# Fourteen seven-product pairs per group in a hybrid decoder layer, with attention work moved into the shared stretch

## The chip, the cores and the metric

The kernel runs on one core of one Trainium2 chip. The metric is the device time of one execution in microseconds (us): 1808.11 us is the median of three runs before (1805.93 to 1808.54). Engines are named as in the profile: PE is TensorE (PEld its weight loads), DVE VectorE, ACT ScalarE, POOL GpSimd, SP SyncE, whose queue issues nearly all transfers.

## The reference

One decoder layer on 256 tokens and 16 prepended meta tokens (272 rows), model width 4096, all in 32-bit floats:

```python
h = rmsnorm(x, norm_g)                        # (272, 4096)
q, k, v, g_attn, b, c, hc, z = split(h @ w_in)  # w_in (4096, 16384)
o = stick_breaking_attention(q, k, v)         # 16 heads of 128, strictly causal
o = group_rmsnorm(o * silu(g_attn), ...)      # per head
y = b * short_conv(c * hc, conv_w)            # width 3, causal
y = group_rmsnorm(y * silu(z), ...)           # per channel group
out = rmsnorm(x + concat(o, y) @ w_out, final_norm_g)   # w_out (4096, 4096)
```

In the attention a query t gives key s the weight sigmoid(z_ts) times the product over the keys between them of (1 - sigmoid), summed up in log space. Nearly all of the arithmetic is the two projections.

## The kernel before, in words

**Numbers.** Every 32-bit operand is split into a high part (a cast to the fast matmul format, on ScalarE) and a low part (operand minus high part, on VectorE), and a product is three matmuls: high by low, high by high, low by high. Weights arrive by DMA as pieces of 128 x 1024 (512 KB, tile `raw`, five buffers); `split` makes `wh` (L401) and `wl` (L397) of each, in rings of six buffers (`RING`), five pieces ahead of TensorE; `load` issues transfers eight pieces ahead. A cast into the ring therefore waits until TensorE has finished the piece six before it.

**Pieces and groups.** The list `pieces` is the order of the work, written out by `in_pieces` and the loop behind it. The input projection goes in eight groups, each of two heads and two channel groups. Of the eight kinds of columns four (k, v, c, hc) are made with the weights standing and the tokens moving: a block `("p", (unit, kind), kc)` of four pieces of 24 matmuls over 272 or 258 columns (L434 to L436), accumulated in one PSUM bank. The other four (q, g_attn, b, z) are made as a 2 x 2 block product: tokens split in two halves, columns in two halves of 512, and the 32 chunks of the width taken as 16 pairs j. A plain pair has two pieces A and B, eight products, 24 matmuls of 512 columns (L442 to L445), accumulated in four banks D11, D12, D21, D22. A shared pair (`seven`) uses a seven-product scheme of the Strassen kind: 21 matmuls, in four pieces A, B, T, U, where T and U are sums of weight halves that VectorE makes (L418, L421, L423) and that are split as well; it accumulates into D11, D12, D21 and four more banks P1, P5, P7, P6. It also needs split sums of the tokens: those of the pairs in `HELD` stay in SBUF, those of `LENT` are made once in group 0 (`late_sums`), stored to DRAM, and read back in every group into two buffers (`lent`).

**Stretches.** A group begins with a plain stretch (zone "R"): its plain pairs, with the last blocks of the group before in between. The four extra banks are then free for the attention of the group before (`spare`). Then D22 is complete and copied out (`open_rows`), and the shared stretch (zone "S") follows: shared pairs, each with half a block behind it, all eight banks in use but the one that D22 left, which holds the block in progress (`block_bank`) and, between two blocks, one other product. Group 0 has plain pairs only. At the end of a group `evict` combines the eight banks into four row tiles.

**Tasks.** Everything else is a task at a position in the list of pieces: `later(at, fn)` files it and `run_tasks(i)` emits it behind piece i, so each engine's queue order is written out by hand. A task that yields k continues k pieces later. `plan_group` places, for group g with f its last block piece in the shared stretch: the gates (`silu`), the transposes of q (`q_t`), `scores`, and for each of two heads `weights` (logarithms, scans, exponentials), `trans` (a transpose in 32 x 32 blocks on VectorE, then sixteen copies of 32-row blocks by `blocks`, alternately on ScalarE and VectorE, L575 and L573) and `po` (the product with v, then an eviction on VectorE); and in the shared stretch of the next group, at `slot`s (piece B of a shared pair), the convolution's transposes (`conv_t`, `conv_out`), `squares`, `norm` and `mix`, which scales, transposes and stores the mixed rows to DRAM.

**Output projection.** Four groups (8 to 11) of 1024 columns (the last 768) are made the same way from the mixed rows, which come back from DRAM as pieces `("m", group)`; `MIXED` and `OUT_FIRST` say where. Their shared pairs are 8 to 13 (the first group: 8 to 11), and the token sums for them are made by `kept_sums`, with the four sums on GpSimd (L308 to L311) in `raw_sums`. `out_sums` and `out_blocks` add the products to the residual rows and square them. The last 256 columns are pieces `("o", 8, kc)` (L933 to L935), then the final norm (`finish`).

Of the kernel before, what the change touches and what calls it, by code (L numbers as in the profile page):

```python
# [15 lines left out]
P = 128  # L16
# [34 lines left out]
MIXED = {(1, "A"): 2, (3, "A"): 3, (5, "A"): 4, (6, "B"): 5, (9, "A"): 6}  # L51
# [7 lines left out]
def sevens(g):  # L59

    return OUT_SJ[:4] if g == GROUPS else OUT_SJ if g > GROUPS else SJ if g else ()

# [5 lines left out]
def in_pieces():  # L68
# [14 lines left out]
    first = ((0, 0), (0, 1), (0, 2), (0, 3), (1, 0), (1, 1))  # L83
    last = ((1, 2), (1, 3))
# [17 lines left out]
    for i, t in enumerate(blocks_of(GROUPS - 1, last)):  # L102
        block(*t)
        if i in (1, 3):
            out.append(("m", i // 2))
# [9 lines left out]
def kernel(ctx, tc, xt, xin, xm, par, fg, w1, w2, out):  # L115
# [23 lines left out]
    ones = wk.tile([P, P], F32, tag="zl", name="ones")  # L139
# [23 lines left out]
    for g in range(GROUPS, GROUPS + 4):  # L163
        for at_, j in enumerate(OUT_ORDER if g > GROUPS else OUT_FIRST):
            for q in "ABTU" if seven(g, j) else "AB":
                pieces.append((q, g, j))
                if g == GROUPS and (at_, q) in MIXED:
                    pieces.append(("m", MIXED[at_, q]))
        fin[g] = len(pieces) - 1
# [111 lines left out]
    def late_sums(j):  # L281
# [6 lines left out]
        yield 2  # L288
# [6 lines left out]
    def kept_sums(d, t, j):  # L295

        f = raw_sums(t, f"o{j}")
        yield 2
# [4 lines left out]
    def raw_sums(t, j):  # L303
# [3 lines left out]
        v = nc.gpsimd  # L307
# [23 lines left out]
    def load(i):  # L331
# [16 lines left out]
        elif p[0] == "m":  # L348
# [12 lines left out]
    def split(i):  # L361
# [9 lines left out]
        if p[0] == "m":  # L371
            t = raws.pop(i).rearrange("p (a b) -> p a b", a=4)
            h, lo = mixh[p[1]], mixl[p[1]]
            nc.scalar.copy(out=h, in_=t)
            for q in range(2):
                j = 2 * p[1] + q
                if j in OUT_SJ:
                    if j < 12:
                        S2[j] = fgs["pool"].tile([P, 2, 4, P], F32R, tag=f"keep{j - 8}", name=f"osum{j}")
                    else:  # L380
                        S2[j] = wk.tile([P, 2, 4, P], F32R, tag="cq" if j == 12 else "cb0", name=f"osum{j}")
                    later(now[0], kept_sums, S2[j], t[:, 2 * q:2 * q + 2], j)
# [95 lines left out]
    def mm_in(i):  # L478
        p = pieces[i]
        if p[0] in "xm":  # L480
            return
# [16 lines left out]
    def block_bank(i):  # L498
# [5 lines left out]
        if kind == "Z":  # L504
            return d + 2 * ((2 * u + b) % 2)
        return d + D22 if g else (4, 5, 6, 0, 1, 2)[{(0, 0): 0, (0, 1): 1, (0, 2): 2, (0, 3): 3, (1, 0): 4, (1, 1): 5}[u, b]]

    def spare(i):
# [5 lines left out]
        if kind == "Z":  # L514
            return [d + 3, d + 1]
# [22 lines left out]
    def finish_stats():  # L538
# [13 lines left out]
        x, y, t = (wk.tile([P, L], F32, tag=q, name=f"st{q}", bufs=2 if q == "u2" else 1) for q in ("u2", "zl", "kT1"))  # L552
# [11 lines left out]
    def blocks(dst, src, n, half):  # L564
# [3 lines left out]
        for i in (0, 1) if half == 0 else (2, 3):  # L568
            for j in range(4):
                o = d[32 * j:32 * j + 32, :, 32 * i:32 * i + 32]  # L570
                x = s[32 * i:32 * i + 32, :, 32 * j:32 * j + 32]
                if (i + j) % 2:
                    V.tensor_copy(out=o, in_=x)  # L573
                else:
                    A.copy(out=o, in_=x)  # L575
# [9 lines left out]
    def v_block(u, src, at_):  # L585
# [4 lines left out]
        def vtrans():  # L590
# [4 lines left out]
            blocks(vv, y[:, :2 * P], 2, 0)  # L595
            yield 1
            blocks(vv, y[:, :2 * P], 2, 1)
# [12 lines left out]
    def h_block(u, src, at_):  # L610
# [3 lines left out]
        def conv():  # L614
            V.tensor_tensor(out=c, in0=c, in1=rstd[:, META - 2:], op=ALU.mult)
            y = wk.tile([P, SEQ], F32, tag=f"cy{u % 2}", name=f"cy{u}")
            w = [pt[:, CW0 + 3 * u + i:CW0 + 3 * u + i + 1] for i in range(3)]
            V.tensor_scalar(out=y, in0=c[:, 0:SEQ], scalar1=w[0], scalar2=None, op0=ALU.mult)
# [6 lines left out]
    def plain_block(u, b, e):  # L625
# [7 lines left out]
        else:  # L633
            h_block(u, ps[:, META - 2:L], after(e, 1))
# [110 lines left out]
    def scores(g):  # L745
# [8 lines left out]
        for u in range(2):  # L754
            zm[u] = (wk.tile([P, 512], F32, tag="u2", name=f"zm{g}_{u}", bufs=2) if u else
                     wk.tile([P, 448], F32, tag="zm", name=f"zm{g}_{u}"))[:, :ZW]
            l[u] = wk.tile([P, 448], F32, tag="kT0" if u else "zl", name=f"zl{g}_{u}")[:, :ZW]
# [86 lines left out]
    def plan_group(g):  # L844
# [4 lines left out]
        later(after(f, 1), q_t, g)  # L849
        later(after(f, 2), silu, g, "c")  # L850
        later(after(f, 3), scores, g)
        for u, at_ in enumerate(((6, 8, 11), (8, 10, 14))):
            for k, fn in zip(at_, (weights, trans, po)):
                later(after(f, k), fn, g, u)
        later(after(f, 16), squares, g, "h")
        if end:
            later(after(e, 4), conv_t, (2 * g, 2 * g + 1))
            later(after(e, 6), conv_out, g)
            later(after(f, 17), squares, g, "c")
            later(after(f, 18), norm, g)  # L860
            later(after(f, 20), mix, g, "h")
            later(after(f, 21), mix, g, "c")
# [133 lines left out]
    for q, j in enumerate(LENT):  # L996
        later(after(top[0], 3 * q + 1), late_sums, j)
# [148 lines left out]
```

## Time and profile before

| | |
|---|---|
| median of three runs | 1808.11 us |
| the profiled execution, its own time | 1808.45 us |
| its span, first to last instruction | 1806.7 us |
| granted TensorE clock, mean | 0.996 |
| PE, DVE, ACT, POOL busy | 99%, 86%, 62%, 8% |
| matmuls of the blocks (L434 to L436) | 6144 |
| moved by DMA | 393.64 MB |

A row of a group of instructions reads: line, engine, operation, tile written <- tiles read, shape, count | busy us, mean ns of one | idle time of the engine before them and what ended it. A row of a timeline reads: start, length, engine and line, with the idle time before it in brackets. A row of waits reads: total us, times, longest. A row of stretches gives the length, the busy time of each engine with its instructions in brackets, the granted clock as a share of full speed, and the DMA's share and rate. Matmuls are pipelined, so that the length of one is more than the step to the next.

### The profile page before, as it was taken

How to read it: one execution, taken by the hardware profiler on the slowest of the kernel's cores; microseconds unless marked ns; L12 is line 12 of the kernel's file. 1: busy time of each engine (PE TensorE's matmuls, PEld its weight loads, DVE VectorE, ACT ScalarE, POOL GpSimd, SP SyncE). 2: the span in 40 equal slices, each digit the busy share in tenths (PEclk: the TensorE clock that was granted, in tenths of full speed). 3: DMA queues.
4: the chain of work that ended last, by engine and by line, in shares of the span. 5: the costliest groups of instructions: out<-in, count | busy, mean ns of one | idle time of the engine just before them, and what ended most of it. 6: DMA issues, size and time to landing. Idle time of an engine off the chain costs nothing.

```text
span 1806.7 us, 29670 instructions
## 1 busy us (share of the span) xinstructions
PE 1784.4 (99%) x11004; PEld 1618.5 (90%) x11004; DVE 1555.5 (86%) x2104; ACT 1120.3 (62%) x1736; POOL 144.5 (8%) x192
## 2 busy tenths in 40 slices
PE   9999999999999999999999999999999999999996
PEld 7899999999998999899999999999999987888896
DVE  6776899889988998899889988998899889898985
ACT  6755666666676667566756575667566765555553
POOL 2132010001000101010101010101010142000000
PEclk9999999999999999999999999999999999999998
DMA  8876567756775676567656765676567666676664
GB/s 311 310 255 209 176 210 236 229 176 212 236 229 172 215 243 211 184 216 236 212 185 216 240 218 172 215 244 218 171 220 244 208 209 238 200 242 213 203 221 162
DMA packets 116065, 393.64 MB, mean 218 GB/s; under 512 B 13008, under 2 KB 18256, under 8 KB 115920
## 3 DMA queue, kind: packets, MB, share of 16 engines
q1 hardware_dynamic: 111888, 388.08, 65.0%
q10 hardware_dynamic: 4032, 3.67, 0.6%
q8 instruction: 86, 1.41, 0.3%
q14 instruction: 59, 0.48, 0.1%
HBM read 380.17 MB, written 11.53 MB: 217 GB/s over the span
## 4 chain that ended last, share of the span: by engine, by line
PE 93%; DVE 3%; ACT 1%; POOL 1%; DMA 1%; issue 1%; SPq 0%; DVEq 0%; POOLq 0%; ACTq 0%
PE P L442 16%; PE P L445 16%; PE P L444 16%; PE mm L436 13%; PE mm L435 13%; PE mm L434 13%; DVE wl L397 1%; DMA raw<-w 1%; ACT wh L401 1%; PE mo L933 0%; PE mo L935 0%; PE mo L934 0%; POOL sfo L308 0%; PE z L752 0%; PE po L808 0%
## 5 line engine op out<-in xcount | busy, mean ns | idle before, releaser
L397 DVE TENSOR_TENSOR wl<-raw,wh 128x1024 fp32r<-128x1024 f32 (+2 forms) x754 | 849.3, 1147 | 121.6 <-ACT wh L401 110.8
L401 ACT CAST wh<-raw 128x1024 fp32r<-128x1024 f32 (+2 forms) x754 | 714.1, 976 | 379.6 <-PE mm L435 109.4
L434 PE MATMUL mm<-xs,wh 128*128 128x258 f32 (+1 forms) x2048 | 582.7, 285 | 0.0
L435 PE MATMUL mm<-xs,wh 128*128 128x258 f32 (+1 forms) x2048 | 581.8, 284 | 0.0
L436 PE MATMUL mm<-xs,wl 128*128 128x258 f32 (+1 forms) x2048 | 581.6, 284 | 0.0
L435 PEld LDWEIGHTS mm<-xs,wh 128*128 128x128 f32 x2048 | 385.6, 188 | 4.1
L434 PEld LDWEIGHTS mm<-xs,wh 128*128 128x128 f32 x2048 | 385.5, 188 | 4.1
L436 PEld LDWEIGHTS mm<-xs,wl 128*128 128x128 f32 x2048 | 385.6, 188 | 0.0
L442 PE MATMUL P<-wh,xs 128*128 128x512 f32 x604 | 238.6, 395 | 1.5 <-ACT wh L401 1.5
L445 PE MATMUL P<-wl,xs 128*128 128x512 f32 x604 | 235.5, 390 | 0.2
L444 PE MATMUL P<-wh,xs 128*128 128x512 f32 x604 | 235.4, 390 | 0.0
L401 ACT CAST wh<-t 128x1024 fp32r<-128x1024 f32 (+1 forms) x106 | 110.4, 1042 | 171.7 <-DVE t L418 97.3
L442 PE MATMUL P<-wh,mixl 128*128 128x512 f32 (+1 forms) x402 | 152.2, 379 | 2.5 <-ACT wh L401 2.5
L445 PE MATMUL P<-wl,mixh 128*128 128x512 f32 (+1 forms) x402 | 151.8, 378 | 0.5 <-DVE wl L397 0.5
L444 PE MATMUL P<-wh,mixh 128*128 128x512 f32 (+1 forms) x402 | 151.5, 377 | 0.0
L445 PEld LDWEIGHTS P<-wl,xs 128*128 128x128 f32 x604 | 113.4, 188 | 25.2 <-DVE wl L397 1.1
L442 PEld LDWEIGHTS P<-wh,xs 128*128 128x128 f32 x604 | 113.5, 188 | 22.7 <-ACT wh L401 1.8
L444 PEld LDWEIGHTS P<-wh,xs 128*128 128x128 f32 x604 | 113.5, 188 | 19.5
L418 DVE TENSOR_TENSOR t<-raw,raw 128x1024 f32<-128x1024 f32 (+1 forms) x106 | 129.7, 1223 | 0.2
L397 DVE TENSOR_TENSOR wl<-t,wh 128x1024 fp32r<-128x1024 f32 (+1 forms) x106 | 129.6, 1222 | 0.0
L442 PEld LDWEIGHTS P<-wh,mixl 128*128 128x128 f32 x402 | 75.7, 188 | 15.1 <-ACT wh L401 3.0
L445 PEld LDWEIGHTS P<-wl,mixh 128*128 128x128 f32 x402 | 75.7, 188 | 13.2 <-DVE wl L397 1.3
(248 smaller groups left out, 2017.8 us busy)
## 6 DMA issues: line engine op xcount, KB each, us to landing
raw<-w SPq DMA_DIRECT2D x614, 512.0 KB, 4.3
lent<-sumd SPq DMA_DIRECT2D x49, 512.0 KB, 6.0
raw<-w SPq DMA_DIRECT2D x32, 384.0 KB, 3.9
raw<-xin SPq DMA_DIRECT2D x8, 512.0 KB, 5.7
xr<-xt SPq DMA_DIRECT2D x15, 272.0 KB, 5.5
sumd<-lent SPq DMA_DIRECT2D x7, 512.0 KB, 4.3
raw<-mixd SPq DMA_DIRECT2D x7, 512.0 KB, 4.1
res<-xin SPq DMA_DIRECT2D x12, 256.0 KB, 4.8
```

The costliest lines, as they stand in the source:

```text
L397: nc.vector.tensor_tensor(out=lo[:, c], in0=t[:, c], in1=h[:, c].bitcast(F32), op=ALU.subtract)
L401: nc.scalar.copy(out=h[:, c], in_=t[:, c])
L418: nc.vector.tensor_tensor(out=s[:, :2 * hw].rearrange("p (a b) -> p a b", a=2), in0=a[:, :2 * hw].rearrange("p (a b) -> p a b", a=2), in1= ...
L434: nc.tensor.matmul(out=o, lhsT=h, rhs=x[:, 0, s:], start=k == 0, stop=False)
L435: nc.tensor.matmul(out=o, lhsT=h, rhs=x[:, 1, s:], start=False, stop=False)
L436: nc.tensor.matmul(out=o, lhsT=lo, rhs=x[:, 0, s:], start=False, stop=k == KC - 1)
L442: nc.tensor.matmul(out=o, lhsT=a[1], rhs=h, start=key not in begun, stop=False)
L444: nc.tensor.matmul(out=o, lhsT=a[0], rhs=h, start=False, stop=False)
L445: nc.tensor.matmul(out=o, lhsT=a[0], rhs=lo, start=False, stop=last)
```

## The change

- Groups 1 to 7 make 14 of the 16 pairs shared instead of 12: pairs 3 and 9 join, in `LENT`, and the order `SJ` of the shared pairs changes. The plain stretch has two plain pairs (0 and 12) instead of four. In the first output group two pairs (9, 10) are shared instead of four.
- Seven of a group's eight blocks (instead of six) lie in its shared stretch, one in the next plain stretch. The scores' logarithm of the second head has a buffer of its own (`zl1` for `kT0`).
- `plan_group`: q's transposes and the scores come one piece later; the first head's weights and transpose stay near, the second head's weights come at f+9; both products `po`, the second head's `trans` and the squares of the attention's half go to slots of the next shared stretch, in the free bank; convolution, norm and mixing move to later slots. The last group has its own places.
- `blocks` copies one 32-column quarter per piece, on ScalarE alone, for v and for the weights (the last group's weights: both engines, two quarters at once). The convolution's first multiply goes from VectorE to ScalarE, and of even units the convolution starts eight pieces after its block.
- The sums of the mixed rows for the output's shared pairs are made on VectorE (`raw_sums(..., V)`). The sums of pairs 12 and 13 are made in the second output group from a second load of mixed rows 6 (piece "k").
- The output groups have an order each (`OUT_ORDERS`); the mixed rows and the residual are loaded at other places. The sums for lent pairs start 2.5 instead of 3 pieces apart, and their cast comes one piece later.

```diff
-LENT = (2, 5, 8, 11, 14, 15, 6)
-SJ = (2, 1, 5, 4, 8, 7, 11, 10, 14, 13, 15, 6)
-OUT_ORDER = (0, 1, 2, 3, 8, 4, 9, 5, 10, 6, 11, 7, 12, 13, 14, 15)
-OUT_FIRST = (0, 1, 2, 3, 4, 5, 6, 8, 7, 9, 14, 10, 15, 11, 12, 13)
+LENT = (2, 5, 8, 11, 14, 15, 6, 3, 9)
+SJ = (2, 1, 5, 4, 8, 11, 7, 14, 15, 10, 6, 13, 3, 9)
+OUT_ORDERS = (
+    (0, 1, 2, 3, 4, 5, 6, 7, 8, 9, 12, 14, 10, 15, 11, 13),
+    (0, 1, 2, 3, 8, 4, 9, 5, 10, 6, 11, 7, 12, 14, 13, 15),
+    (0, 1, 8, 2, 9, 3, 10, 4, 11, 5, 12, 6, 13, 7, 14, 15),
+    (0, 1, 8, 2, 9, 3, 10, 4, 11, 5, 12, 6, 13, 7, 14, 15),
+)
-MIXED = {(1, "A"): 2, (3, "A"): 3, (5, "A"): 4, (6, "B"): 5, (9, "A"): 6}
+MIXED = {(0, "A"): 1, (1, "B"): 2, (3, "A"): 3, (6, "B"): 4, (7, "B"): 6, (10, "A"): 5}
...
-    return OUT_SJ[:4] if g == GROUPS else OUT_SJ if g > GROUPS else SJ if g else ()
+    return OUT_SJ[1:3] if g == GROUPS else OUT_SJ if g > GROUPS else SJ if g else ()
...
-    first = ((0, 0), (0, 1), (0, 2), (0, 3), (1, 0), (1, 1))
-    last = ((1, 2), (1, 3))
+    first = ((0, 0), (0, 1), (0, 2), (0, 3), (1, 0), (1, 1), (1, 2))
+    last = ((1, 3),)
...
     def kept_sums(d, t, j):
-        f = raw_sums(t, f"o{j}")
-        yield 2
+        f = raw_sums(t, f"o{j}", V)
+        yield 1
...
-    def blocks(dst, src, n, half):
+    def blocks(dst, src, n, i, engines):
...
-        for i in (0, 1) if half == 0 else (2, 3):
-            for j in range(4):
-                o = d[32 * j:32 * j + 32, :, 32 * i:32 * i + 32]
-                x = s[32 * i:32 * i + 32, :, 32 * j:32 * j + 32]
-                if (i + j) % 2:
-                    V.tensor_copy(out=o, in_=x)
-                else:
-                    A.copy(out=o, in_=x)
+        for j in range(4):
+            e = engines[(i + j) % len(engines)]
+            e(out=d[32 * j:32 * j + 32, :, 32 * i:32 * i + 32], in_=s[32 * i:32 * i + 32, :, 32 * j:32 * j + 32])
...
-            blocks(vv, y[:, :2 * P], 2, 0)
-            yield 1
-            blocks(vv, y[:, :2 * P], 2, 1)
+            for i in range(4):
+                blocks(vv, y[:, :2 * P], 2, i, (A.copy,))
+                yield 1
...
-            V.tensor_scalar(out=y, in0=c[:, 0:SEQ], scalar1=w[0], scalar2=None, op0=ALU.mult)
+            A.mul(out=y, in_=c[:, 0:SEQ], mul=w[0])
+            yield 1
...
-            h_block(u, ps[:, META - 2:L], after(e, 1))
+            h_block(u, ps[:, META - 2:L], after(e, 1 if u % 2 else 8))
...
-        blocks(at[:, P:], y[:, :3 * P], 3, 0)
-        yield 1
-        blocks(at[:, P:], y[:, :3 * P], 3, 1)
+        for i in range(4):
+            blocks(at[:, P:], y[:, :3 * P], 3, i, (A.copy,) if g < GROUPS - 1 else (A.copy, V.tensor_copy))
+            if i < 3 and (g < GROUPS - 1 or i == 1):
+                yield 1
...
-        later(after(f, 1), q_t, g)
+        later(after(f, 2), q_t, g)
         later(after(f, 2), silu, g, "c")
-        later(after(f, 3), scores, g)
-        for u, at_ in enumerate(((6, 8, 11), (8, 10, 14))):
-            for k, fn in zip(at_, (weights, trans, po)):
-                later(after(f, k), fn, g, u)
-        later(after(f, 16), squares, g, "h")
+        later(after(f, 4), scores, g)
+        later(after(f, 7), weights, g, 0)
+        later(after(f, 9), weights, g, 1)
+        later(after(f, 9), trans, g, 0)
...
-        later(slot(g + 1, 2), conv_t, (2 * g, 2 * g + 1))
-        later(after(slot(g + 1, 2), 2), conv_out, g)
-        later(slot(g + 1, 5), squares, g, "c")
-        later(slot(g + 1, 6), norm, g)
-        later(slot(g + 1, 8), mix, g, "h")
-        later(slot(g + 1, 10), mix, g, "c")
+        t = [slot(g + 1, c) for c in range(len(SJ))]
+        later(t[2], po, g, 0)
+        later(after(t[2], 1), trans, g, 1)
+        later(t[4], po, g, 1)
+        later(t[5], squares, g, "h")
+        later(t[6], conv_t, (2 * g, 2 * g + 1))
+        later(after(t[6], 2), conv_out, g)
+        later(after(t[7], 2), squares, g, "c")
+        later(t[8], norm, g)
+        later(t[10], mix, g, "h")
+        later(t[12], mix, g, "c")
```

More of the change, by code (lines that the diff above doesn't have):

```diff
@@ L136, in bank @@
         return pp.tile([P, 512], F32, tag=f"b{i}", name=nm)
-    ones = wk.tile([P, P], F32, tag="zl", name="ones")
+    ones = wk.tile([P, P], F32, tag="zl0", name="ones")
     nc.vector.memset(ones, 1.0 / P)
@@ L163 @@
     for g in range(GROUPS, GROUPS + 4):
-        for at_, j in enumerate(OUT_ORDER if g > GROUPS else OUT_FIRST):
+        for at_, j in enumerate(OUT_ORDERS[g - GROUPS]):
             for q in "ABTU" if seven(g, j) else "AB":
@@ L168 @@
                     pieces.append(("m", MIXED[at_, q]))
+                if g == GROUPS + 1 and (at_, q) == (4, "A"):
+                    pieces.append(("k", 6))
         fin[g] = len(pieces) - 1
@@ L370, in split @@
             return
-        if p[0] == "m":
+        if p[0] in "mk":
             t = raws.pop(i).rearrange("p (a b) -> p a b", a=4)
+            if p[0] == "k":
+                for q in range(2):
+                    S2[12 + q] = wk.tile([P, 2, 4, P], F32R, tag="cb0" if q else "cq", name=f"osum{12 + q}")
+                    later(now[0], kept_sums, S2[12 + q], t[:, 2 * q:2 * q + 2], 12 + q)
+                return
             h, lo = mixh[p[1]], mixl[p[1]]
@@ L376, in split @@
                 j = 2 * p[1] + q
-                if j in OUT_SJ:
-                    if j < 12:
-                        S2[j] = fgs["pool"].tile([P, 2, 4, P], F32R, tag=f"keep{j - 8}", name=f"osum{j}")
-                    else:
-                        S2[j] = wk.tile([P, 2, 4, P], F32R, tag="cq" if j == 12 else "cb0", name=f"osum{j}")
+                if j in OUT_SJ and j < 12:
+                    S2[j] = fgs["pool"].tile([P, 2, 4, P], F32R, tag=f"keep{j - 8}", name=f"osum{j}")
                     later(now[0], kept_sums, S2[j], t[:, 2 * q:2 * q + 2], j)
@@ L504, in block_bank @@
         if kind == "Z":
-            return d + 2 * ((2 * u + b) % 2)
-        return d + D22 if g else (4, 5, 6, 0, 1, 2)[{(0, 0): 0, (0, 1): 1, (0, 2): 2, (0, 3): 3, (1, 0): 4, (1, 1): 5}[u, b]]
+            return d
+        return d + D22 if g else (4, 5, 6, 0, 1, 2, 4)[4 * u + b]
     def spare(i):
@@ L551, in finish_stats @@
         V.tensor_scalar(out=m, in0=ss[:, :L], scalar1=1.0 / 32.0, scalar2=None, op0=ALU.mult)
-        x, y, t = (wk.tile([P, L], F32, tag=q, name=f"st{q}", bufs=2 if q == "u2" else 1) for q in ("u2", "zl", "kT1"))
+        x, y, t = (wk.tile([P, L], F32, tag=q, name=f"st{q}", bufs=2 if q == "u2" else 1) for q in ("u2", "zl0", "kT1"))
         u = rsqrt_raw(m, L, EPS, x, y, t)
@@ L996 @@
     for q, j in enumerate(LENT):
-        later(after(top[0], 3 * q + 1), late_sums, j)
+        later(after(top[0], 5 * q // 2 + 1), late_sums, j)
     tasks.sort(key=lambda t: t[0])
@@ L1052 @@
                 later(i + 1, out_sums, g)
-            if p[0] == "B" and p[2] in (10, 6):
-                load_res(2 * (g - GROUPS) + (p[2] == (6 if g > GROUPS else 10)))
+            for q, j in enumerate((12, 14) if g == GROUPS else (10, 6)):
+                if p[0] == "B" and p[2] == j:
+                    load_res(2 * (g - GROUPS) + q)
             if i == fin[g]:
@@ L1114 @@
         hw = hwid(GROUPS + c // 1024)
-        for j in OUT_ORDER if c else OUT_FIRST:
+        for j in OUT_ORDERS[c // 1024]:
             m1, m2 = w[2 * j], w[2 * j + 1]
```

39 lines of the change are left out of this document (21 added, 18 removed).

## The prediction

> **What bounds the kernel now.** I read the page's engine totals and its chain of waits first, then TensorE's own waits.
>
> ```profile
> span 1806.7 us, 29670 instructions
> PE 1784.4 (99%) x11004; PEld 1618.5 (90%) x11004; DVE 1555.5 (86%) x2104; ACT 1120.3 (62%) x1736; POOL 144.5 (8%) x192
> ...
> PE 93%; DVE 3%; ACT 1%; POOL 1%; DMA 1%; issue 1%; SPq 0%; DVEq 0%; POOLq 0%; ACTq 0%
> ```
>
> ```profile
> PE P L442 <- ACT wh L401: 4.0, 2, 2.5
> PE mo L933 <- DVE res L908: 2.8, 1, 2.8
> PE qT L741 <- DVE vt L588: 1.7, 3, 1.2
> PE warm L143 <- DVE ones L140: 1.1, 1, 1.1
> PE P L445 <- DVE wl L397: 1.1, 2, 0.6
> ```
>
> TensorE is the bound in nearly the whole span: its waits add to 10.7 us of 1806.7. Time can leave in two ways only: fewer matmuls, or fewer of those few microseconds. It can come back in one way: VectorE at 86% falls behind somewhere and makes TensorE wait. So I price the matmuls, then the waits, then VectorE's reserve in each stretch.
>
> **The matmuls removed.** Groups 1 to 7 turn two more pairs each from eight products to seven (14 pairs), and the first output group turns two back (four to two): net 12 pairs, each 21 matmuls of 512 columns instead of 24. That is 36 matmuls fewer. What one costs is the step between starts, in the timeline of TensorE through one plain piece of twelve:
>
> ```profile
> 1529.69 0.39 PE L442 MATMUL P<-wh,mixl 128*128 128x512 f32 x1
> ...
> 1532.41 0.39 PE L442 MATMUL P<-wh,mixl 128*128 128x512 f32 x1
> ```
>
> 2.72 us for twelve is 0.227 us each (0.39 is the pipelined length, not the cost). 36 x 0.227 = 8.2 us off the path.
>
> **VectorE's bill.** The views are groups of instructions by line, and busy time by stretch (length, then PE, PEld, DVE, ACT, POOL, granted clock, DMA share, GB/s). The first two stretches are one shared pair with its half block each; the first is quiet, the second carries attention work. The third is the first half of a plain stretch, the last is a whole group.
>
> ```profile
> 762.40:773.08 10.68, 10.68 (x71) 9.86 (x70) 9.07 (x9) 5.68 (x6) 0.00 (x0) 1.00 0.62 201
> 826.42:836.92 10.50, 10.50 (x71) 9.66 (x70) 10.37 (x11) 6.03 (x7) 0.00 (x0) 1.00 0.62 201
> 836.92:848.08 11.16, 11.16 (x75) 10.26 (x74) 10.91 (x15) 6.53 (x8) 0.00 (x0) 1.00 0.77 258
> 880.62:904.88 24.26, 24.26 (x159) 22.15 (x158) 20.50 (x34) 20.74 (x39) 5.51 (x8) 1.00 0.60 193
> 880.62:1058.70 178.08, 178.08 (x1159) 163.48 (x1158) 157.90 (x214) 114.10 (x182) 10.42 (x14) 1.00 0.65 213
> ```
>
> ```profile
> L397 DVE TENSOR_TENSOR wl<-raw,wh 128x1024 fp32r<-128x1024 f32 (+2 forms) x754 | 849.3, 1147 | 121.6 <-ACT wh L401 110.8
> L575 ACT COPY at<-ya 32x96 f32<-32x96 f32 x128 | 34.4, 269 | 26.0 <-PE po L807 23.4
> L575 ACT COPY vv<-yv 32x64 f32<-32x64 f32 x128 | 31.0, 242 | 1.5
> L573 DVE COPY at<-ya 32x96 f32<-32x96 f32 x128 | 27.7, 217 | 19.5 <-PE po L807 16.6
> L573 DVE COPY vv<-yv 32x64 f32<-32x64 f32 x128 | 27.4, 214 | 2.3
> L618 DVE TENSOR_SCALAR cy<-cc,pt 128x256 f32<-128x256 f32 x16 | 5.7, 353 | 0.6
> L615 DVE TENSOR_TENSOR cc<-cc,rstd 128x258 f32<-128x258 f32 x16 | 6.8, 424 | 0.3
> ```
>
> A quiet shared pair with two block pieces takes 9.07 us of VectorE; less two subtractions of 1.147 for the blocks, 6.78. A plain pair is two subtractions, 2.29. So a pair made shared costs 4.49 more, 12 of them 53.9 us. Against that, the small copies leave: all 27.4 us of vv, and seven groups of eight of at (24.2; the last group keeps both engines), and the first multiply of the convolution, 5.7. The kept sums come to VectorE: 6 x 4 subtractions and additions of 128x128, which no row shows there; they lie between nothing and the 0.424 of 128x258, 0 to 10.2 us, and I take two thirds of the upper end, 0.28 each, 6.7 us. Net +3.3 us: 1559 us of some 1790, 87%, so VectorE as a whole is no more loaded than before. ScalarE gets 112 copies of 0.269 and 128 of 0.242 (61 us) and about 1.5 casts per pair: it stays under 70%. The two added sums per group are also read back (14 transfers of 512 KB); the stretch at 836.92 moved 258 GB/s with no TensorE wait, and a shared pair with such a read asks about five half megabytes in 10.6 us, 247 GB/s. I cost these transfers at nothing, and with them two more stores in group 0 and one reload in the second output group; the cover is that SyncE issues each read eight pieces ahead, and if it were gone the matmuls on the sums would wait for the landing.
>
> **Where it is tight: from the plain stretch into the shared one.** The plain stretch halves to two pairs and one block, and the second head's weights and both transposes move past its end. The rows that carry the walk, from VectorE's timeline (rows of eviction, z mask and weights):
>
> ```profile
> 876.23 0.69 DVE L653 TENSOR_TENSOR cb<-P,cq 128x512 f32<-128x512 f32 x1 [0.38 <-ACT cq L652]
> ...
> 880.56 0.68 DVE L660 TENSOR_TENSOR cb<-P,cb 128x512 f32<-128x512 f32 x1
> ...
> 897.61 0.59 DVE L773 SCALAR_TENSOR_TENSOR zs<-zm,zl 128x416 f32<-128x416 f32 x1 [0.73 <-ACT zl L767]
> ...
> 899.35 0.59 DVE L777 TENSOR_TENSOR zs<-zm,zl 128x416 f32<-128x416 f32 x1
> ```
>
> The eviction takes 5.0 us, one head's weights 2.3. The half stretch before (880.62 to 904.88) already held the z masks and one head's weights and kept VectorE 20.5 of 24.3 us busy, of which eight copies of 0.214, 1.7, leave; the new plain stretch fits inside the old half. After it, two shared pairs ask 2 x 9.07 + 2.3 (second weights) + a transpose, two multiply-adds and two tiny copies, which I put at the weights' 2.3 again (five short instructions against their four) = 22.7 us in 21.4 of TensorE. That deficit of 1.3 us is paid from the lead that six split buffers give. What lead suffices, the trace shows at its thinnest, in the slot that runs into 826.42, VectorE then TensorE:
>
> ```profile
> 824.68 1.22 DVE L397 TENSOR_TENSOR wl<-t,wh 128x1024 fp32r<-128x1024 f32 x1
> ```
>
> ```profile
> 828.93 0.39 PE L445 MATMUL P<-wl,sum 128*128 128x512 f32 x1
> ```
>
> Ready at 825.90, used at 828.93: 3 us in hand, followed by two slots at 98 to 99% VectorE and no wait. Taking off the deficit, and the copies that now stand in front of ScalarE's casts (four of 0.269 per piece, 1.1 us), about half a microsecond to one stays in hand. Every pair after it gives back 1.6. So I forecast no regular wait, and put 2 us in the sum for stray ones. Ends: 0, and 2.5 us in each of seven groups (17.5).
>
> The bank shared by the blocks, the two attention products, the convolution's transposes and the mixing is already used this way by three of these five, one piece after a block ends, and no row of TensorE's waits names po, ct or mx. I cost two more uses at nothing; a wait would be the DVE eviction that is late, some 0.5 us each.
>
> **The waits that go.** In the first output group the chain runs through GpSimd's sums:
>
> ```profile
> 1490.34 4.85 POOL L308 TENSOR_TENSOR sfo<-raw 128x128 f32<-128x128 f32 x1 [8.62 <-DVE wl L397]
> ```
>
> ```profile
> 1487.97 4.62 DVE L397 TENSOR_TENSOR wl<-raw,wh 128x1024 fp32r<-128x1024 f32 x4
> ```
>
> ```profile
> 1501.04 0.62 ACT L299 CAST osum<-sfo 128x512 fp32r<-128x512 f32 x1 [2.58 <-POOL sfo L311]
> ```
>
> ```profile
> 1498.93 0.50 PE L445 MATMUL P<-wl,osum 128*128 128x512 f32 x1 [0.55 <-DVE wl L397]
> 1502.65 0.50 PE L442 MATMUL P<-wh,mixl 128*128 128x512 f32 x1 [2.52 <-ACT wh L401]
> ```
>
> ```profile
> 1503.90:1507.30 3.40, 3.39 (x8) 2.64 (x9) 3.40 (x4) 2.20 (x3) 0.00 (x0) 0.53 0.96 308
> 1770.30:1773.70 3.40, 2.94 (x14) 2.94 (x14) 3.40 (x8) 2.42 (x4) 0.00 (x0) 0.51 0.01 2
> ```
>
> ScalarE's cast waits for a GpSimd sum, the pieces behind it are late, TensorE waits 0.55, 2.52 and once more 0.5 us. Then it is granted half its clock: eight matmuls in 3.4 us that would take 8 x 0.227, 1.6 us lost. Sum 5.2. With sums of 0.28 us on VectorE and one shared pair instead of two by that point, all of it goes; nothing else late stands there, as the plain pieces ahead leave VectorE 2.29 of 5.44 us.
>
> At the tail, VectorE then TensorE:
>
> ```profile
> 1768.52 1.23 DVE L397 TENSOR_TENSOR wl<-raw,wh 128x1024 fp32r<-128x1024 f32 x1 [1.06 <-ACT wh L401]
> 1770.14 0.56 DVE L908 TENSOR_TENSOR res<-P,res 128x384 f32<-128x384 f32 x1 [0.40 <-ACT os L907]
> ```
>
> ```profile
> 1770.76 0.58 PE L933 MATMUL mo<-keep,mixl 128*128 128x256 f32 x1 [2.79 <-DVE res L908]
> ...
> 1773.70 0.33 PE L934 MATMUL mo<-keep,mixh 128*128 128x256 f32 x1
> ```
>
> The last block waits for a bank that L908 reads, and L908 stands behind casts that wait for buffers. The new order puts one more plain pair (24 matmuls of 384 columns, some 0.17 us each by the 0.227 of 512, so 4.1 us) between the last shared pair and this point, more than the 2.8 waited. The 13 slow steps after it (0.226 us against about 0.12 for 256 columns, a little over half of 0.227) cost 1.4. Sum 4.2. The product of q's transposes is moved one piece later, past the v eviction that it waited for: 1.7 more.
>
> The sum against this execution's 1808.45 us (1.75 around its span; the median of the runs is 0.3 lower): 1808.45 - 8.2 - 5.2 - 4.2 - 1.7 = 1789.2, with 2 for stray waits **1791 us**.
>
> A rule stands against part of this. The Trainium skill, in "TensorE: Matmul & The Clock Gate", section "Part 1: The HAM clock gate", lets the clock fall to half only after an idle window of about 3.4 us. Here it stood at half after idle times of 2.52 and 2.79 us. By the page the slow matmuls would not be the waits' doing and the 3.0 us would stay, 1794; the two rows side by side speak for the wait as the cause.
>
> **The rivals.** *Lead lost, slower.* If VectorE and ScalarE come 4 us later than my walk at the start of each shared stretch, TensorE waits 2.5 us there, and the 2.52 above was enough to halve the clock, 1.6 more: 4.1 x 7 = 28.7, 1789.2 + 28.7 = 1818. For it: slots at 98% exist already, and ScalarE's queue is in order, so copies or exponentials that wait hold up casts. Against: the copies' own waits for the product (26.0 us of idle before L575) go, since the second head's copies now come a piece after that product. It turns to a loss from 2.75 us per group on (19.2 over 7).
>
> *Lead grazed.* The same place, 1 to 2 us per group and the clock kept: 1796 to 1803.
>
> *Waits stay.* The output stage is late because of the transfers and the mixing's splits, and the tail for its buffers: only 8.2 and 1.7 go, with the 2 stray us 1800.6. For it: ScalarE also waits for landing pieces there. Against: the 2.58 ends at a sum.
>
> *It does not do what it says.* The matmuls go but VectorE's 87% spreads badly, and each group ends as long as before: within a few us of 1808.
>
> **How the numbers follow.** Forecast (1786 to 1796) 0.60; grazed 0.13; waits stay 0.12; as long as before 0.05; slower 0.10. The range of 1786 to 1802 holds the first three nearly whole: the lower end is the sum with no stray wait and three us more, the upper end grazing at 1.8 us a group. Changes under 0.2% (3.6 us) can't be told here: faster 0.85, same 0.05, slower 0.10.
>
> **What would show it.** Right: the step of a whole group falls from 178.1 to 176.7 us; TensorE's waits lose L908, L741 and the osum rows and keep 1.5 us of L442 at the start; no clock below 1 between start and tail. Wrong: waits of L442 or L445 on wh or wl that recur seven times, one per group just after the plain stretch; po, ct or mx among TensorE's waits; VectorE over 1600 us.

## The result, and the profile after

The changed kernel takes 1818.35 us (median of four runs, 1816.98 to 1819.97) beside 1807.3 us for the kernel before (four runs of the same series): a ratio of 1.0062, interval 1.0044 to 1.0079. It is slower by 11 us where 1791 was forecast, and outside the range of 1786 to 1802.

The head of the page after, and TensorE's waits (us in total, times, longest):

```profile
span 1818.2 us, 29724 instructions
...
PE 1794.0 (99%) x10968; PEld 1622.2 (89%) x10968; DVE 1561.5 (86%) x1936; ACT 1211.2 (67%) x2018; POOL 132.6 (7%) x176
```

```profile
PE mm L441 <- DVE cq L664: 7.8, 6, 1.4
PE P L449 <- ACT wh L408: 1.6, 1, 1.6
PE warm L147 <- DVE ones L144: 1.1, 1, 1.1
PE mm L441 <- ACT wh L408: 1.0, 1, 1.0
PE po L808 <- DVE kT L584: 0.3, 2, 0.2
PE po L808 <- DVE at L577: 0.2, 1, 0.2
```

TensorE has 36 matmuls fewer and is busy 9.6 us longer. The waits that were to go have gone: L908, the qT row, the osum rows. VectorE's total came out as forecast: 1561.5 for 1559. What is new is the wait of one product (L441), for the eviction of the bank D11 (L664) in six groups, 7.8 us, and for a late cast at the same place in the first, 1.0 us. That leaves most of the distance to the forecast without a wait.

Where it lies shows from the starts of the first and last of seven like pieces, pair 0 of groups 1 and 7 (six group steps apart), before and then after:

```profile
172.35 0.40 PE L442 MATMUL P<-wh,xs 128*128 128x512 f32 x1
...
1244.22 0.39 PE L442 MATMUL P<-wh,xs 128*128 128x512 f32 x1
```

```profile
186.75 0.48 PE L449 MATMUL P<-wh,xs 128*128 128x512 f32 x1
...
1274.24 0.48 PE L449 MATMUL P<-wh,xs 128*128 128x512 f32 x1
```

A group takes (1244.22 - 172.35) / 6 = 178.64 us before and 181.25 after: 2.61 more, where six matmuls fewer should have made it 1.36 less. (The forecast's 178.1 was a single group cut at another point; measured this way its 176.7 reads 177.28.) The output stage, in contrast, from the first output piece to the end, before and after:

```profile
1442.70:1806.70 364.00, 346.27 (x1696) 299.57 (x1694) 308.74 (x405) 196.85 (x277) 30.66 (x29) 0.98 0.62 210
```

```profile
1462.60:1818.20 355.60, 343.74 (x1702) 298.48 (x1700) 308.04 (x430) 202.85 (x289) 4.41 (x8) 0.99 0.65 217
```

It is 8.4 us shorter, six matmuls that came back included; the forecast's terms for it give 5.2 + 4.2 - 1.4 = 8.0. So the groups of the input projection are the place. The groups of matmuls by shape show what happened there. Before, then after (busy us, mean ns of one | idle time before them):

```profile
L434 PE MATMUL mm<-xs,wh 128*128 128x272 f32 x1024 | 293.5, 287 | 0.0
L435 PE MATMUL mm<-xs,wh 128*128 128x272 f32 x1024 | 293.4, 287 | 0.0
L436 PE MATMUL mm<-xs,wl 128*128 128x272 f32 x1024 | 293.4, 287 | 0.0
```

```profile
L441 PE MATMUL mm<-xs,wh 128*128 128x272 f32 x1024 | 296.7, 290 | 0.0
L442 PE MATMUL mm<-xs,wh 128*128 128x272 f32 x1024 | 296.6, 290 | 0.0
L443 PE MATMUL mm<-xs,wl 128*128 128x272 f32 x1024 | 296.6, 290 | 0.0
```

The same 3072 matmuls take 3 ns more each, and none waits. Two pieces of one block, 48 such matmuls, undisturbed (length, then PE, PEld, DVE, ACT, POOL, clock, DMA share, GB/s), before and after:

```profile
778.34:784.26 5.92, 5.92 (x49) 5.92 (x48) 5.89 (x6) 2.99 (x3) 3.01 (x5) 1.00 0.52 183
```

```profile
777.03:783.11 6.08, 6.08 (x50) 6.07 (x48) 4.94 (x6) 5.89 (x14) 0.00 (x0) 1.00 0.69 235
```

5.92 us have become 6.08 at full clock: a step of 126.7 ns instead of 123.3. Over the 3072 matmuls that is 10 us; no edit of the change touches these instructions. The other shapes slow down too, by less: by the starts in the traces, the mean step, waits left out, of the 258-column matmuls goes from 119.3 to 119.9 ns (3072 of them, 2 us) and that of the 512-column ones from 227.3 to 228.7 (some 3700, 5 us). Two things differ around them: ScalarE, GpSimd and the DMA queues do other work (5.89 us of ScalarE beside them instead of 2.99), and the tiles lie elsewhere. The new buffer `zl1` makes the working tiles 1088 bytes larger, so what lies behind them, the weight pieces, the split weight tiles and the token sums, moves up by 1088 bytes, while the token tiles `xs`, laid out from the other end, stay. By the kernel's allocation `xs` and the split weight tiles stood 1216 bytes apart modulo 2048; now it is 128.

### The profile page after: what moved, and what is told of

It is laid out like the page before. It is cut to its first block, busy times and chain, and to the rows that moved or that the text cites. A ratio compares the mean times of both kernels' runs of the same rounds, so it can differ in the third digit from the quotient of the medians.

```text
span 1818.2 us, 29724 instructions
## 1 busy us (share of the span) xinstructions
PE 1794.0 (99%) x10968; PEld 1622.2 (89%) x10968; DVE 1561.5 (86%) x1936; ACT 1211.2 (67%) x2018; POOL 132.6 (7%) x176
## 4 chain that ended last, share of the span: by engine, by line
PE 88%; DVE 4%; ACT 4%; issue 2%; DMA 2%; ACTq 0%; DVEq 0%; SPq 0%
PE P L449 16%; PE P L451 16%; PE P L452 16%; PE mm L441 12%; PE mm L443 12%; PE mm L442 12%; ACT wh L408 2%; DVE wl L404 2%; DMA raw<-w 1%; ACT vv L577 1%; PE mo L947 0%; PE mo L945 0%; PE mo L946 0%; PE po L812 0%; PE z L756 0%
## 5 line engine op out<-in xcount | busy, mean ns | idle before, releaser
L404 DVE TENSOR_TENSOR wl<-raw,wh 128x1024 fp32r<-128x1024 f32 (+3 forms) x766 | 864.4, 1151 | 157.4 <-ACT wh L408 145.2
L408 ACT CAST wh<-raw 128x1024 fp32r<-128x1024 f32 (+3 forms) x766 | 723.1, 973 | 318.3 <-PE mm L442 88.4
L441 PE MATMUL mm<-xs,wh 128*128 128x258 f32 (+1 forms) x2048 | 589.9, 288 | 8.8 <-DVE cq L664 7.8
L441 PEld LDWEIGHTS mm<-xs,wh 128*128 128x128 f32 x2048 | 385.4, 188 | 15.9 <-ACT wh L408 10.1
L408 ACT CAST wh<-t 128x1024 fp32r<-128x1024 f32 (+1 forms) x118 | 123.2, 1044 | 171.3 <-DVE t L425 123.9
L449 PE MATMUL P<-wh,xs 128*128 128x512 f32 x534 | 211.5, 396 | 1.6 <-ACT wh L408 1.6
L451 PE MATMUL P<-wh,xs 128*128 128x512 f32 x534 | 210.4, 394 | 0.0
L452 PE MATMUL P<-wl,xs 128*128 128x512 f32 x534 | 209.1, 392 | 0.0
L449 PE MATMUL P<-wh,mixl 128*128 128x512 f32 (+1 forms) x412 | 155.8, 378 | 0.0
L452 PE MATMUL P<-wl,mixh 128*128 128x512 f32 (+1 forms) x412 | 155.0, 376 | 0.0
L404 DVE TENSOR_TENSOR wl<-t,wh 128x1024 fp32r<-128x1024 f32 (+1 forms) x118 | 144.1, 1221 | 6.2 <-ACT wh L408 6.2
L425 DVE TENSOR_TENSOR t<-raw,raw 128x1024 f32<-128x1024 f32 (+1 forms) x118 | 144.0, 1220 | 0.0
L452 PEld LDWEIGHTS P<-wl,xs 128*128 128x128 f32 x534 | 100.6, 188 | 23.1
L449 PEld LDWEIGHTS P<-wh,xs 128*128 128x128 f32 x534 | 100.7, 189 | 19.9 <-ACT wh L408 1.9
L451 PEld LDWEIGHTS P<-wh,xs 128*128 128x128 f32 x534 | 100.9, 189 | 16.8
L449 PE MATMUL P<-wh,lent 128*128 128x512 f32 x252 | 101.1, 401 | 0.0
L451 PE MATMUL P<-wh,lent 128*128 128x512 f32 x252 | 98.7, 392 | 0.0
```

What stands on the lines that cost most here:

```text
L404: nc.vector.tensor_tensor(out=lo[:, c], in0=t[:, c], in1=h[:, c].bitcast(F32), op=ALU.subtract)
L408: nc.scalar.copy(out=h[:, c], in_=t[:, c])
L425: nc.vector.tensor_tensor(out=s[:, :2 * hw].rearrange("p (a b) -> p a b", a=2), in0=a[:, :2 * hw].rearrange("p (a b) -> p a b", a=2), in1= ...
L441: nc.tensor.matmul(out=o, lhsT=h, rhs=x[:, 0, s:], start=k == 0, stop=False)
L449: nc.tensor.matmul(out=o, lhsT=a[1], rhs=h, start=key not in begun, stop=False)
L451: nc.tensor.matmul(out=o, lhsT=a[0], rhs=h, start=False, stop=False)
```

## The experiments

All times are medians in us; the ratio is to runs of the kernel before in the same series. The step is a group's, read as above.

| kernel | time | ratio, interval | group step |
|---|---|---|---|
| before | 1806 to 1807 | | 178.64 |
| after | 1818.35 | 1.0062 (1.0044 to 1.0079) | 181.25 |
| e1 before, token tiles shifted | 1822.88 | 1.0092 (1.0077 to 1.0107) | 180.71 |
| e2 after, 192 bytes apart | 1802.85 | 0.998 (0.997 to 0.9989) | 179.10 |
| e3 after, 64 bytes apart | 1816.91 | 1.0058 (1.0041 to 1.0075) | 180.65 |
| e4 after, convolution early | 1816.48 | 1.0057 (1.0042 to 1.0072) | 180.57 |
| e5 = e2, eviction's copy first | 1801.81 | 0.997 (0.9958 to 0.9981) | 178.94 |
| e6 = e2, product one piece later | 1823.69 | 1.0093 (1.0072 to 1.0114) | 182.61 |
| e7 = e5 and e6 | 1821.51 | 1.0078 (1.0062 to 1.0093) | 182.11 |
| e8 = e7, 256 bytes apart | 1837.11 | 1.0163 (1.0148 to 1.0178) | 183.49 |
| e9 = e5, v copies behind the eviction | 1794.03 | 0.993 (0.9915 to 0.9944) | 178.00 |
| e10 = e9, products two pairs later | 1836.19 | 1.0164 (1.0129 to 1.0199) | 183.79 |
| e11 before, output part alone | 1799.76 | 0.9962 (0.9949 to 0.9975) | 178.64 |
| e12 = e9, k eviction first | 1791.87 | 0.992 (0.9903 to 0.9936) | 177.66 |

### Placement alone, both ways: e1, e2, e3

The theory: the slower pace is the tiles' placement. The rival: the load of the other engines.

```diff
 # e1, in the kernel before
-    xp.tile([P, 40], F32, name="pad_x")
+    xp.tile([P, 312], F32, name="pad_x")
 # e2, in the changed kernel (e3: [P, 56])
-    xp.tile([P, 40], F32, name="pad_x")
+    xp.tile([P, 24], F32, name="pad_x")
```

> The kernel before with one change: the pad behind the x tiles grows by 1088 bytes, so the x tiles lie 1088 bytes lower and stand to the split weight tiles (wh, wl) as they do in the changed kernel: 128 bytes apart modulo 2048 instead of 1216. No instruction is added or moved. Placement theory (the slower pace of the 272- and 258-column products in the changed kernel comes from where its tiles lie in SBUF): the 272-column step rises from 123.3 ns to about 126.6, the 258-column one to about 123, and the time from 1807 to 1817-1824. Rival (the pace comes from the changed load of ScalarE, VectorE or the DMA queues): steps and time as before, 1807.

> The changed kernel with the pad behind the x tiles 64 bytes smaller: x tiles and split weight tiles stand 192 bytes apart modulo 1024, as in the kernel before (128 in the changed kernel). Placement theory: the 272-column step falls from 126.6 ns to about 123.3, the waits at the start of the plain stretches stay, time 1818 - 13 = 1805 (1802 to 1808). Rival (load of the other engines): 1818 and the same steps.

> The changed kernel with the pad 64 bytes larger: 64 bytes apart instead of 128. Placement theory, if what counts is the distance modulo 128 (64 in the kernel before, 0 in the changed one): as e2, 1805. If it is the distance modulo 256 or more: some third pace, between 1805 and 1825. Rival (load): 1818.

The kernel before slows down to 1822.88, and its rows become those of the changed kernel (the 258-column step, expected at 123 ns, only goes to 119.9 there as well). The group of one line and the stretch of two block pieces, of e1 and then of e2:

```profile
L434 PE MATMUL mm<-xs,wh 128*128 128x272 f32 x1024 | 296.7, 290 | 0.0
```

```profile
788.10:794.18 6.08, 6.08 (x50) 6.08 (x49) 6.05 (x6) 3.02 (x3) 3.04 (x5) 1.00 0.43 150
```

```profile
L441 PE MATMUL mm<-xs,wh 128*128 128x272 f32 x1024 | 293.5, 287 | 0.0
```

```profile
769.02:774.94 5.92, 5.92 (x49) 5.91 (x48) 4.80 (x6) 5.73 (x14) 0.00 (x0) 1.00 0.69 233
```

An unused pad, with every instruction where it was, makes the block's two pieces 6.08 us in the kernel before; a pad smaller by 64 bytes makes them 5.92 in the changed one, with ScalarE and the DMA as busy as ever. The rival is out. The pad moves the `xs` tiles alone, so their place against everything else is what costs; which of the other tiles matters, the three runs don't separate. The 64 bytes are worth 1818.35 - 1802.85 = 15.5 us (14.9 with each held against its own series of the kernel before), and the changed kernel then beats the one before. e3 says that the distance modulo 128 is not what counts: 64 bytes apart is about as slow as 128, and the group steps say the same (180.65).

### The eviction at the end of the shared stretch: e4, e5, e9

In e2 the row of the eviction is still there, at 0.9 us per group with its restart. Where TensorE starts on the block behind the last product, before and after:

```profile
874.70 0.29 PE L434 MATMUL mm<-xs,wh 128*128 128x272 f32 x1
```

```profile
898.21 0.28 PE L441 MATMUL mm<-xs,wh 128*128 128x258 f32 x1
```

ScalarE, VectorE and TensorE of the changed kernel around it:

```profile
889.99 1.01 ACT L577 COPY vv<-yv 32x64 f32<-32x64 f32 x4
891.02 1.06 ACT L408 CAST wh<-raw 128x1024 fp32r<-128x1024 f32 x1
892.10 1.01 ACT L577 COPY vv<-yv 32x64 f32<-32x64 f32 x4
893.13 1.05 ACT L408 CAST wh<-raw 128x1024 fp32r<-128x1024 f32 x1
894.09 0.90 ACT L602 COPY v<-yv 16x32 f32<-16x32 f32 x4
895.01 3.91 ACT L408 CAST wh<-raw 128x1024 fp32r<-128x1024 f32 x4
899.90 1.06 ACT L408 CAST wh<-raw 128x1024 fp32r<-128x1024 f32 x1 [0.99 <-DMA raw<-w]
900.87 0.57 ACT L656 COPY cq<-P 128x512 f32<-128x512 f32 x1
```

```profile
896.10 4.63 DVE L404 TENSOR_TENSOR wl<-raw,wh 128x1024 fp32r<-128x1024 f32 x4 [0.65 <-ACT wh L408]
901.47 0.69 DVE L657 TENSOR_TENSOR cb<-P,cq 128x512 f32<-128x512 f32 x1 [0.74 <-ACT cq L656]
```

```profile
905.43 0.36 PE L441 MATMUL mm<-xs,wh 128*128 128x258 f32 x1 [1.30 <-DVE cq L664]
```

The eviction starts at 901.47, 3.26 us after the last product; before it was 876.23 - 874.70 = 1.53 (the 876.23 stands in the prediction). And the two pieces that TensorE has meanwhile are of 258 columns now, not of 272. Ahead of it stand the odd head's v copies: the block of v is no longer the last of the shared stretch but the last but one, so its copies now run before the eviction instead of after it. The next block waits for D11.

```diff
 # e4, in the changed kernel
-            h_block(u, ps[:, META - 2:L], after(e, 1 if u % 2 else 8))
+            h_block(u, ps[:, META - 2:L], after(e, 1))
 # e5, on e2: in evict ScalarE's copy is taken out; where a piece is made, ahead of the casts:
+        if i in top.values() and p[1]:
+            open_cq(p[1])        # cq tile, A.copy(out=cq[:, 0], in_=psum.pop((g, P1)))
...
 # e9, on e5, in vtrans behind the transpose
-            yield 1
+            yield 11 if u % 2 and u > 1 else 1
```

> The changed kernel with the v step of the even head (its eviction, transpose and ScalarE copies) one piece after its block instead of eight, so that its copies no longer stand on ScalarE at the end of the shared stretch. Theory for the wait at the start of each plain stretch: the vv copies push ScalarE's casts, and behind them the copy that the eviction needs, late; without them there the wait of 1.46 us in seven groups goes, 1818 - 10 = 1808. Rival (VectorE's own load or the reads of the weights make the eviction late): the wait stays, 1818. The pace of the matmuls stays at 126.6 ns under both.

The edit missed its aim: the line is that of the convolution's step of the even head, and the v copies stayed. At 1816.48 it tells nothing about them. The row of L664 did shrink in its trace, to 4.2 us in seven groups, and the cast ahead of the eviction's copy waited 0.25 us for its weight piece in the same group instead of the 0.99 above; e5 takes the copy out from behind that cast.

> e2 (x tiles 192 bytes from the weight tiles) with one copy moved: ScalarE's copy of the product bank P1, with which the eviction at the end of each shared stretch begins, is issued ahead of the casts of the next split piece instead of behind them. Theory (the eviction starts late because that copy stands in ScalarE's queue behind a cast that waits for a weight piece to land, after the odd head's v copies have taken ScalarE's lead): the wait of 0.4 to 1.4 us at the start of each plain stretch goes, 7 x 0.8 = 5.6 us, 1803 - 5.6 = 1797. Rival (VectorE itself is late there, its subtractions stand ahead of the eviction): the wait stays, 1803.

> e5 with the odd head's v copies (12 of 32x64 and 4 of 16x32 on ScalarE) put behind the eviction instead of ahead of it, from group 1 on. Theory (these copies spread ScalarE's casts at the end of the shared stretch, VectorE's four subtractions behind them run into the eviction and start it 2.5 us after the last product where the kernel before takes 1.5): the wait at the start of the plain stretch goes, 7 x 0.73 = 5.1 us, 1802 - 5.1 = 1796.7. Rival (the eviction has become too slow for the two 258-column blocks that now stand there, 5.6 us instead of 5.9): at least half of the wait stays, 1799 or more.

e5 put the copy at 887.02, where the next block starts at 887.30, and gained only about 1 us: the eviction started at 889.80, behind four subtractions. So of e5's two theories the rival holds: the copy's place in ScalarE's queue was not what came last. In e9 the copies are gone from there. VectorE and TensorE of e9:

```profile
880.60 4.88 DVE L404 TENSOR_TENSOR wl<-raw,wh 128x1024 fp32r<-128x1024 f32 x4 [1.63 <-ACT wh L408]
885.40 0.68 DVE L662 TENSOR_TENSOR cb<-P,cq 128x512 f32<-128x512 f32 x1
```

```profile
884.21 0.29 PE L441 MATMUL mm<-xs,wh 128*128 128x258 f32 x1
```

The eviction starts 1.19 us after the last product there, and no wait for it is left in any group. 1801.81 became 1794.03: 7.8 us for the 5.1 expected (6.6 by the group step); what the rest was is open. That the copies were the cause is shown; the rows say how: they had spread ScalarE's casts, and VectorE's subtractions behind these came late, one link further up than e5 had sought it.

### The shared bank: e6, e7, e8, e10, e12

At the right pace another row comes up. TensorE's waits in e2 and then in e6:

```profile
PE po L808 <- DVE kT L584: 3.9, 7, 0.6
```

```profile
PE mm L441 <- DVE cq L816: 19.2, 7, 2.8
```

The first attention product of a shared stretch stands at its third pair, in the bank that VectorE has yet to empty of the k block. e6 and e10 move the product; e12 moves the emptying.

```diff
 # e6 (e7: on e5), in plan_group
-        later(t[2], po, g, 0)
-        later(after(t[2], 1), trans, g, 1)
+        later(after(t[2], 1), po, g, 0)
+        later(after(t[2], 2), trans, g, 1)
 # e8, on e7
-    xp.tile([P, 24], F32, name="pad_x")
+    xp.tile([P, 8], F32, name="pad_x")
 # e10, on e9, in plan_group (conv_out, trans and squares move with them)
-        later(t[2], po, g, 0)
-        later(t[4], po, g, 1)
-        later(t[6], conv_t, (2 * g, 2 * g + 1))
+        later(t[0], conv_t, (2 * g, 2 * g + 1))
+        later(t[4], po, g, 0)
+        later(t[6], po, g, 1)
 # e12, on e9, where a piece is made, ahead of the casts
+        first = i > top[0] + 1 and p[0] == "p" and p[2] == 3 and p[1][1] == 0
+        if first:
+            plain_block(*p[1], i)
...
```

> e2 with the first head's attention product, and the second head's transpose behind it, one piece later in the shared stretch (after the third product of the pair instead of the second). Theory (the product waits for its bank, which VectorE has not yet emptied of the k block): the wait on kT, 0.56 us and the restart behind it, 0.8 per group, goes: 1803 - 5.6 = 1797. Rival (the bank is only handed on: the next block of k and v products, two pieces later, now waits for the product's own eviction): the wait moves to the 258- or 272-column products, 1803.

> e2 with the copy of e5 and the product of e6. If the slower pace, the late eviction and the shared bank are all that stood between the forecast and the time: 1803 - 11 = 1792 (1790 to 1794), and the step of a whole group 177.2 us or less. If something else takes their place: 1796 or more.

The rival, and worse than it: 1823.69 and 1821.51. TensorE and VectorE of e6, where the product's own eviction (L816) is now what is late:

```profile
777.25 0.39 PE L452 MATMUL P<-wl,lent 128*128 128x512 f32 x1
780.37 0.36 PE L441 MATMUL mm<-xs,wh 128*128 128x272 f32 x1 [2.73 <-DVE cq L816]
...
784.77 0.43 PE L441 MATMUL mm<-xs,wh 128*128 128x272 f32 x1
785.00 0.37 PE L442 MATMUL mm<-xs,wh 128*128 128x272 f32 x1
```

```profile
778.66 0.69 DVE L430 TENSOR_TENSOR raw<-raw 128x512 f32<-128x512 f32 x1
779.27 0.64 DVE L797 STREAM_TRANSPOSE ya<-za 128x448 f32<-128x448 f32 x1
779.83 0.38 DVE L816 TENSOR_TENSOR cq<-po,cq 128x256 f32<-128x256 f32 x1
```

L816 stands behind a whole pair's T and U work, and the next block needs the bank. After the wait of 2.73 us the matmuls keep their step of 0.124 us for 1.3 us more; then, until 785.0, they step by 0.23: 1.6 us more at half clock.

> e7 with the pad behind the x tiles 64 bytes smaller again: x tiles and weight tiles 256 bytes apart instead of 192. Distances of 64 and 128 gave a 272-column step of 127.1 ns, 192 gave 123.9 (as 1216 did in the kernel before). If the pace follows the distance modulo 256, 256 is like 0, and 0 lies beside 64: slow, 127, some 13 us more than e7. If it needs a distance of 192 bytes or more: as e7.

15.6 us more than e7: slow, as the modulo-256 reading said. It is not the same slowness, though: here the median step of the 512-column matmuls rises from 227 to 231 ns and that of the 272-column ones only to 125, and in e3 both are slow (231 and 127), in the changed kernel the second alone (227 and 127). (The 127.1 and 123.9 of the expectation are 126.6 and 123.3 as means over whole pieces.) More: at 64 and 256 even products that read no `xs` tile, those on the `sum` tiles, step by 231 ns (median between starts) where the changed kernel has 227, though the pad moved neither their tiles nor the weights'. So the distance between a matmul's own two tiles can't be the whole rule.

> e9 with the attention products two pairs later in the shared stretch (pairs 5 and 7 instead of 3 and 5, the convolution's transposes at the first pair instead of the seventh), so that the bank is asked for where VectorE is ahead again. Theory (the product at the third pair waits because VectorE is then only 3 us ahead and empties the k block late): the wait on kT and the restart behind it go, 7 x 0.83 = 5.8 us: 1791 (1789.5 to 1793.5), the forecast's own time. Rival (the convolution's transposes at the first pair now wait for its bank or its data): waits of ct, 1797 or more.

1836.19, the rival. Both moves met the bank at a bad place, TensorE's waits of e10, and a stretch of eight 512-column matmuls behind one of them:

```profile
PE po L813 <- DVE cc L609: 15.6, 7, 2.2
PE ct L827 <- DVE cy L624: 12.3, 7, 1.8
```

```profile
755.85:758.83 2.98, 2.98 (x8) 2.34 (x7) 2.95 (x3) 1.94 (x7) 2.70 (x3) 0.50 0.56 197
```

The convolution is not ready by the first pair, and at pair 7 the c block is the one that waits to be emptied.

> e9 with VectorE's eviction of each k block issued ahead of the next piece's subtraction instead of behind two of them; nothing else moves. Theory (the first attention product of each shared stretch waits for its bank only because VectorE, without lead there, runs two subtractions of 1.2 us before that eviction): the wait on kT, 0.56 us and the restart behind it, goes: 7 x 0.83 = 5.8 us, 1794 - 5.8 = 1788 (1787 to 1790). Rival (VectorE now stands idle until the block ends, and its subtractions come late for the pair's next products): new waits of L449 or L452 on wl, 1793 or more.

1791.87, 2.2 of the expected 5.8 us. The kT row has gone, and in its place the second product waits for the v block. TensorE's waits of e12:

```profile
PE po L813 <- DVE vt L590: 1.6, 7, 0.5
...
```

It is the fastest version: 0.992 of the kernel before (0.9903 to 0.9936), 1.5% under the changed one. The v block's eviction ahead of its subtractions as well was not tried.

### The output part alone: e11

On the kernel before, with the lines that follow from these (the "k" piece, the loads of the residual) as in the diff of the change, and nothing else:

```diff
+OUT_ORDERS = ( ... )
-MIXED = {(1, "A"): 2, (3, "A"): 3, (5, "A"): 4, (6, "B"): 5, (9, "A"): 6}
+MIXED = {(0, "A"): 1, (1, "B"): 2, (3, "A"): 3, (6, "B"): 4, (7, "B"): 6, (10, "A"): 5}
-    return OUT_SJ[:4] if g == GROUPS else OUT_SJ if g > GROUPS else SJ if g else ()
+    return OUT_SJ[1:3] if g == GROUPS else OUT_SJ if g > GROUPS else SJ if g else ()
-        f = raw_sums(t, f"o{j}")
+        f = raw_sums(t, f"o{j}", V)
...
```

> The kernel before with the change's output part alone: the output orders, the mixing's places, two shared pairs instead of four in the first output group, kept sums on VectorE. The twelve pairs per group, the block order and the copies stay as before. By the forecast's own terms: 9.4 us less for the two waits and the slow clock behind them, 1.4 more for six matmuls that come back (2 x 3 x 0.227): 1807 - 8.0 = 1799. If the output stage keeps its waits (the rival called waits stay): 1807 to 1809.

1799.76, with the group step unchanged at 178.64. The difference of 6.3 us, with the 1.4 for six matmuls more, puts the two removed waits and their slow clock at 7.7 us (by the profiled spans, 1806.7 and 1797.6, at 10.5); the forecast had 9.4. The rival "Waits stay" is out.

## Why the prediction was wrong

**What held.** *VectorE's bill*: 1561.5 us for 1559; a kept sum takes 0.285 to 0.292 us for the 0.28 put on it. *The lead at the start of the shared stretch*: the walk left half a microsecond to one in hand and no regular wait. At the thinnest slot, the second half of the first k block in groups 1 to 7, VectorE has 1.2 to 1.4 us in hand in the changed kernel, and 1.0 in e12 at the right pace. Its subtraction, the first of the two in the row, is ready at 763.23; the piece that needs it starts at 764.22, and its third matmul, at 764.47, is the first to use it:

```profile
762.00 2.36 DVE L404 TENSOR_TENSOR wl<-raw,wh 128x1024 fp32r<-128x1024 f32 x2 [0.92 <-ACT wh L408]
```

```profile
764.22 0.29 PE L441 MATMUL mm<-xs,wh 128*128 128x272 f32 x1
```

So the rival that gave 1818, "Lead lost, slower", named the right time for a cause that isn't there: no row of L449 or L452 recurs per group. *The waits that go*: all gone in the changed kernel, where the output stage is 8.4 us shorter with the six matmuls that came back; its part alone, e11, is worth 6.3 by the medians. *The matmuls removed*: 8.2 us is right as far as the step stays 0.227, which it does in the changed kernel's median. e12, which mends the first two of the three things below and most of the third's wait, lies at 1791.87, at the forecast's own time. That is partly luck: against its own series of the kernel before (1806.62) it gains 14.8 us where the forecast had 17 from 1808.1. Its group step of 177.66 is 0.4 above 177.28; the vt row, 1.6 us over seven groups, explains 0.2 of it.

**The step that failed most** is one that the prediction never wrote down. The sum takes the matmuls that the change leaves alone at their old price ("Time can leave in two ways only ... It can come back in one way: VectorE at 86% falls behind somewhere"). There was another way back: the pace of the blocks' 6144 matmuls, and of the others beside them, depends on where the tiles lie (10 us for the 272 columns, 2 for the 258, 5 for the 512, by the steps above), and a buffer renamed in the attention moved one side. That is 15.5 of the 26.5 us between the changed kernel and e12. It could not be read off the profile of before, which shows one placement only; it could have been suspected from the diff (a new tag in a pool with others behind it) and from unused pads of odd sizes in the kernel.

**The second** is in "Where it is tight". I took the eviction at its length of 5.0 us and walked on from its end; whether it starts on time I did not ask. The block order puts the odd head's v step ahead of it, and the copies that I let lie beside other work on ScalarE ("it stays under 70%") stood in the one queue whose order decided. At the changed kernel's pace this was a wait of 1.0 to 1.4 us in each of seven groups, 8.8 in all and about 10 with the restart behind it; with e2's pace e5 and e9 together took 8.8 out. The share of ScalarE, 67%, was right and answered the wrong question.

**The third**: "I cost two more uses at nothing; a wait would be the DVE eviction that is late, some 0.5 us each." The wait came as 0.56 us in each of seven groups, for one of the two. It hardly shows in the changed kernel (0.3 us in all), where the slow pace probably gives VectorE time, and only comes up once that is mended; e6 and e10 show how close it stands: the product one piece later makes the next block wait 2.7 us, two pairs later it waits 2.2 us itself, and part of these waits is followed by half the clock.

## What to carry to other kernels

Ask of every edit to a buffer which tiles it moves, and hold the mean of a matmul shape that the change doesn't touch against the one before, ahead of any search for waits: three nanoseconds more on every one, without a wait, can be a placement, and an unused pad tells that apart from the load of the other engines. Where work moves across a fixed point such as an eviction, walk the queue up to that point as well as from it. A bank shared by several users has a window, and a user moved within it needs both neighbours' evictions checked.

## What the runs showed of the hardware

A matmul's step depended on where the token tiles lay in SBUF against the other tiles. With the distance to the split weight tiles as the measure, the mean step of a 272-column matmul in undisturbed pieces of 48 was 123.3 ns at 1216 and 192 bytes (modulo 2048), 126.6 at 128 and 64, and 125.3 at 256; the median 512-column step was 227 ns, but 231 at 64 and 256. 192 and 1216 are equal modulo 1024, and modulo 128 can't be it, since 64 is slow and 192 is not. But in the two cases with 231 ns the products on the `sum` tiles were slow as well, whose own tiles had not moved, so that which tiles count, and by what rule, the runs leave open. The Trainium skill, in "SBUF — State Buffer", section "A bandwidth-pool intuition that's wrong (but worth ruling out)", gives TensorE a second, independent read port for loading weights. That alone would not let one expect a dependence on placement; here there is one, of 15.5 us.

The clock again fell to half after short idle times: after 2.73 us in e6, and to 0.50 in the stretch quoted of e10 after a wait of 1.8. It does not always fall: in the profiled executions it fell after six of e6's seven waits of 2.7 us, after five of e10's fourteen of 1.7 to 2.2 us, and after none of the changed kernel's of 1.0 to 1.4. The Trainium skill, in "TensorE: Matmul & The Clock Gate", section "Part 1: The HAM clock gate", asks for an idle window of about 3.4 us; these traces disagree, as the prediction's two rows did.
